# First mixer of a two-block kernel: the order of front, inverse, solve, chain and norm for head pairs 1 to 3

## The chip, the core and the metric

The kernel runs on one core of a Trainium2 chip. The metric is the device time of one execution in microseconds, as the median of several runs; lower is better.

## What is computed

The program runs two transformer blocks over 512 tokens of width 1024. The first block has a mixer (a bidirectional RWKV-7 recurrence over 8 heads of 64, plus a pooling branch) and an expert layer; the second has another mixer and two feed-forward layers. Only the recurrence of the first mixer is touched:

```python
def step(state, inp):
    r_t, w_t, k_t, v_t, kk_t, a_t = inp
    sa = jnp.einsum('bhvk,bhk->bhv', state, -kk_t)
    state = (state * w_t[:, :, None, :]
             + sa[..., :, None] * (kk_t * a_t)[..., None, :]
             + v_t[..., :, None] * k_t[..., None, :])
    out = jnp.einsum('bhvk,bhk->bhv', state, r_t)
    return state, out
```

It is run forward and backward in time (d = 0 and 1), the two outputs are added and normalised per head, a bonus term is added, the sum is gated, and w_out projects the result together with the pooling branch.

## The kernel before, in words

The recurrence is not stepped token by token. The 8 heads are four pairs (i = 0 to 3, two heads of 64 rows in 128 partitions), the 512 tokens are 8 chunks of 64, and each pair goes through five functions:

- `front(i)` (line 348) loads r, k, v of the pair (line 355) and a low-rank weight (line 358), normalises k (`head_scale`, lines 326 to 343: matmuls L330 and L343), makes the decay and the mixing gates (L371, L373), scans the decay within chunks (L385), and for each direction makes scaled copies on VectorE and GpSimd (L392 to L405) and the small products within each chunk on TensorE (L318, called through `mm2`), which VectorE masks into the tiles `gl`, `kc` and `x` (L415, L428). Its last matmul is the bonus term (L431). Its PSUM tiles come from the pool `ppf`, which has two.
- `invert(i)` (line 435) inverts a triangular 64x64 matrix for each chunk, head and direction: a transpose on VectorE (L448), 15 dependent steps of a multiply and an add on VectorE (L469, L470), two more transposes (`dt` L473, `dn` L475), then five groups of small matmuls (L488, L495, L503, L510, L517), each with a ScalarE or VectorE copy before the next can start; the last copy is L521. It starts from `gl`, so from the end of its front. Its tiles (`inv`) and its PSUM tile (`ppi`) exist once.
- `solve(i)` (line 523) turns v (L318 on `v` and `vf`, copied at L537), applies the inverse (`x<-th`, L545), and folds the result into `kc` and `rd` (L551, L557); last comes the part of each chunk that does not depend on the state (L562, L563). PSUM from `ppb`, two tiles.
- `chain(i)` (line 565) carries the state through the 8 chunks: per chunk one matmul group into `pzs`, one VectorE add (L585), one group into `po`. `po` is one of the two `ppb` tiles and is held to the end; `pzs` exists once.
- `back(i)` (line 589) copies `po` (L596), centres and normalises it (L598, `head_scale` again) and applies the gate.

The tiles that a pair carries from one function to the next (`gl`, `rd`, `x`, `kc`, `at`, `th`) live in one of three slots, pair i in slot i % 3. Slots 1 and 2 are opened at lines 624 and 625, after the 20 input projections (`w_in`, matmuls at L141), and closed after `back(2)`. The space they leave is used by the tile `xt` (loads at L643) and by the pool `wp3`: the pooling results `pd` (loads at L666, one buffer, four in turn, each split by ScalarE at L70 and GpSimd at L71), and the weights of the output projection. `project(4, 4)` (line 649) multiplies the four pooling tiles with w_out: 8 output blocks of 12 matmuls, 96 in all, at L141. `solve(3)`, `chain(3)` and `back(3)` are written between the pooling splits and this projection.

The program text is not the order on the engines. A planner lays out each engine's queue ahead of time: an instruction written earlier goes first when it is ready, and one written later fills in when nothing earlier is ready and its tiles are free. What it lays out is then fixed; each engine works through its queue in order. So moving a call in the text moves priorities, and the trace shows what filled in where.

Of the kernel before, what the change touches and what calls it, by code (L numbers as in the profile page):

```python
# [40 lines left out]
def flip(ap):  # L41
    dims = [list(q) for q in ap.ap]
    step, n = dims[-1]
    dims[-1] = [-step, n]
    return bass.AP(tensor=ap.tensor, offset=ap.offset + step * (n - 1), ap=dims)
# [3 lines left out]
def tile_two_blocks(ctx: ExitStack, tc: tile.TileContext, a: dict, out: bass.AP):  # L49
# [15 lines left out]
    def vv(name, j):  # L65
        o = VOFF[name] + j
        return vec[:, o:o + 1]
# [95 lines left out]
    with ExitStack() as c1:  # L163
# [9 lines left out]
        def psb(p=ppb):  # L173
            return p.tile([128, 512], F32, tag="ps", name="ps")
# [133 lines left out]
        def open_slots(n, side):  # L308
            c = c1.enter_context(ExitStack())
            slots[n] = (mk(c, f"slot{n}", 1, side=side), c)  # L310

        def c8(ap):
            return ap.rearrange("p (c t) -> p c t", t=64)

        def mm2(ps, w_, x_, start=True, stop=True):

            for j in (0, 64):
                PE.matmul(ps[j:j + 64], w_[j:j + 64], x_[j:j + 64], start=start, stop=stop, tile_position=(j, j))  # L318

        def c4(ps):  # L320
            return ps.rearrange("p (c t) -> p c t", t=128)
# [4 lines left out]
        def head_scale(pp, sq, eps):  # L326

            ps = psb(pp)
            for t in range(4):
                PE.matmul(ps[:, t * 2:t * 2 + 2], sq[:, t * 128:(t + 1) * 128], cst[:, C_IND:C_IND + 2],  # L330
                          start=True, stop=True)
            rs = tp.tile([128, 2, 8], F32, tag=f"rs{eps is None}", name="rs", bufs=2)
            if eps is None:
                S.activation(rs[:, 0], ps[:, :8], AF.Sqrt)
                V.tensor_scalar(rs[:, 0], rs[:, 0], 1e-12, None, op0=ALU.max)
            else:
                V.tensor_scalar(rs[:, 0], ps[:, :8], 1.0 / 64, eps, op0=ALU.mult, op1=ALU.add)
                S.activation(rs[:, 0], rs[:, 0], AF.Sqrt)
            V.reciprocal(rs[:, 1], rs[:, 0])
            pb = psb(pp)  # L340
            for t in range(4):
                for j in range(2):
                    PE.matmul(pb[j * 64:j * 64 + 64, t * 128:(t + 1) * 128],  # L343
                              rs[:, 1, t * 2 + j:t * 2 + j + 1].to_broadcast([128, 64]), ident,
                              start=True, stop=True)
            return pb
# [176 lines left out]
        def solve(i):  # L523


            qd = Q[i]
            th, gl = qd["th"], qd["gl"]

            vt = qd["vt"] = gl[:, :, :, 64:128]
            vT = rkv["v", i]  # L530
            vf = tp.tile([128, T], F32, tag="vf", name="vf")
            G.tensor_copy(vf, flip(vT))
            for d in range(2):
                p = c8(psb())
                for c in range(8):
                    mm2(p[:, c, :], c8(vf if d else vT)[:, c, :], ident2)
                S.activation(vt[:, d], p, AF.Copy)  # L537
            for d in range(2):
                u = qd[d]
                rd, x_, kc, at_ = u["rd"], u["x"], u["kc"], u["at"]  # L540
                for h in range(2):
                    p = c4(psb())
                    for c in range(4):
                        mm2(p[:, c, :], th[:, h * 4 + c, d, :], x_[:, h * 4 + c, :])
                    S.activation(x_[:, h * 4:h * 4 + 4], p, AF.Copy)  # L545
                for h in range(2):
                    cs_ = slice(h * 4, h * 4 + 4)
                    p = c4(psb())
                    for c in range(4):
                        mm2(p[:, c, :], gl[:, d, h * 4 + c, 0:64], x_[:, h * 4 + c, :])  # L550
                    V.tensor_add(kc[:, cs_], kc[:, cs_], p)  # L551
                    p = c4(psb())
                    c0 = 1 - h
                    cs_ = slice(h * 4 + c0, h * 4 + 4)
                    for c in range(c0, 4):
                        mm2(p[:, c, :], at_[:, h * 4 + c, :], x_[:, h * 4 + c, :])
                    V.tensor_add(rd[:, cs_], rd[:, cs_], p[:, c0:])  # L557

                p = c8(psb())
                for c in range(7):  # L560
                    mm2(p[:, c, :], kc[:, c, 64:128], vt[:, d, c, :])
                S.activation(th[:, 1, d, :], p[:, 0, :], AF.Copy)  # L562
                S.activation(gl[:, d, 1:7, 0:64], p[:, 1:7, :], AF.Copy)  # L563

        def chain(i):
            qd = Q[i]
            th = qd["th"]
            po = qd["po"] = psb()

            def out_(c, d, inter):  # L570
                n = 7 - c if d else c
                r_ = qd[d]["rd" if inter else "kc"][:, c, 0:64]
                mm2(po[:, n * 64:n * 64 + 64], th[:, c, d, :] if inter else qd["vt"][:, d, c, :],
                    flip(r_) if d else r_, start=not inter and c == 0 and d == 0, stop=inter and c == 7 and d == 1)

            for c in range(8):
                for d in range(2):
                    out_(c, d, False) if d == 0 else out_(7 - c, d, False)
            pzs = ppz.tile([128, 2, 2, 64], F32, tag="pz", name="pzs")
            for c in range(7):  # L580
                if c:
                    pz = pzs[:, c % 2]
                    for d in range(2):
                        mm2(pz[:, d], qd[d]["rd"][:, c, 64:128], th[:, c, d, :])
                    V.tensor_add(th[:, c + 1], pz, qd["gl"][:, :, c, 0:64])  # L585
                for d in range(2):
                    out_(c + 1, d, True)

        def back(i):
            qd = Q.pop(i)  # L590
            po = qd["po"]

            gt = tp.tile([128, T], F32, tag="gt", name="gt")
            nc.sync.dma_start(gt, gate_d[i])
            o = yt[i] = yb.tile([128, T], F32, tag="y", name="y") if i < 3 else tp.tile([128, T], F32, tag="nkk", name="y")
            S.activation(o, po, AF.Copy)  # L596
            pb = psb()
            PE.matmul(pb, cst[:, C_CEN:C_CEN + 128], o, start=True, stop=True)  # L598
            S.activation(o, pb, AF.Copy)
            sq = tp.tile([128, T], F32, tag="vf", name="sq")  # L600
            S.activation(sq, pb, AF.Square)
            pb = head_scale(ppb, sq, 64e-5)
            V.tensor_mul(o, o, pb)
            V.tensor_scalar(o, o, vv("ln_x_w", i), vv("ln_x_b", i), op0=ALU.mult, op1=ALU.add)
            V.tensor_add(o, o, qd["bon"])
            V.tensor_mul(o, o, gt)
# [16 lines left out]
        cw.close()  # L623
        open_slots(1, "right")
        open_slots(2, "right")
        front(1)
        invert(1)
        front(2)
        solve(1)
        chain(1)  # L630
        invert(2)
        back(1)
        front(3)
        solve(2)
        chain(2)
        invert(3)
        back(2)
        slots[2][1].close()
        slots[1][1].close()
        xp = mk(cx1, "xp3", 1, side="right")  # L640
# [832 lines left out]
```

## Time and profile before

| what | value |
|---|---|
| median of 3 runs | 3052.63 us (3047.12 to 3056.36) |
| profiled execution | 3042.29 us, span 3040.5 us |
| TensorE busy over the span | 2877.7 us (95%) |
| VectorE busy over the span | 1896.8 us (62%) |
| stretch of pairs 1 to 3, up to the end of `project(4, 4)` | about 223 to 443 us |
| TensorE busy in that stretch | 188.15 of 220 us |

All times in views are microseconds from the span's start. PE is TensorE, PEld its weight loads, DVE VectorE, ACT ScalarE, POOL GpSimd, SP the queue that issues most DMAs. A tile such as `ps<-x,th` reads: the matmul wrote ps from x and th. "[idle before <-X]" is how long the engine stood still before the row and what ended that. The granted clock (PEclk) is 1.00 at the full 2.4 GHz and 0.50 at 1.2 GHz; between them it is a mean over the stretch.

### The profile page before, as it was taken

How to read it: one execution, taken by the hardware profiler on the slowest of the kernel's cores; microseconds unless marked ns; L12 is line 12 of the kernel's file. 1: busy time of each engine (PE TensorE's matmuls, PEld its weight loads, DVE VectorE, ACT ScalarE, POOL GpSimd, SP SyncE). 2: the span in 40 equal slices, each digit the busy share in tenths (PEclk: the TensorE clock that was granted, in tenths of full speed). 3: DMA queues.
4: the chain of work that ended last, by engine and by line, in shares of the span. 5: the costliest groups of instructions: out<-in, count | busy, mean ns of one | idle time of the engine just before them, and what ended most of it. 6: DMA issues, size and time to landing. Idle time of an engine off the chain costs nothing.

```text
span 3040.5 us, 45240 instructions
## 1 busy us (share of the span) xinstructions
PE 2877.7 (95%) x17733; PEld 2402.8 (79%) x17733; DVE 1896.8 (62%) x3317; ACT 1198.8 (39%) x2073; POOL 924.9 (30%) x584
## 2 busy tenths in 40 slices
PE   8897898999989799999999999999999999999998
PEld 6676776799989677799999977888876666788886
DVE  7567638899987377777777786332258744643311
ACT  6344334237867233333333334332234343433322
POOL 1011135211321111133444324444431233244443
PEclk9899989999999899999999999999999999999999
DMA  3240123257876699999899962333321112323332
GB/s 115 63 129 27 41 77 122 70 164 257 315 271 241 239 303 318 311 327 306 307 315 332 313 218 63 97 97 95 99 93 49 56 56 66 101 91 97 97 96 78
DMA packets 201286, 494.92 MB, mean 163 GB/s; under 512 B 17328, under 2 KB 95152, under 8 KB 199152
## 3 DMA queue, kind: packets, MB, share of 16 engines
q1 hardware_dynamic: 164208, 357.78, 36.0%
q0 software_dynamic: 36864, 134.23, 12.7%
q8 instruction: 140, 2.29, 0.3%
q14 instruction: 74, 0.61, 0.1%
HBM read 446.60 MB, written 45.22 MB: 162 GB/s over the span
## 4 chain that ended last, share of the span: by engine, by line
PE 59%; DVE 21%; issue 7%; ACT 4%; DMA 4%; POOL 2%; SPq 0%; ACTq 0%; DVEq 0%; POOLq 0%
PE ps L141 33%; PE pss L731 8%; PE pv L1043 8%; DVE vl L978 2%; DVE row L756 2%; ACT vh L972 2%; DVE o L913 2%; PE ps L318 2%; DVE ul L71 2%; DMA gate<-gates_d 2%; DMA uraw<-peer_ut 1%; PE po L1287 1%; DVE st L983 1%; PE pg L920 1%; PE ps L1263 1%
## 5 line engine op out<-in xcount | busy, mean ns | idle before, releaser
L71 POOL TENSOR_TENSOR wlo<-wraw,whi 128x1024 fp32r<-128x1024 f32 (+4 forms) x232 | 503.6, 2174 | 775.9 <-ACT whi L70 773.7
L70 ACT ACTIVATE whi<-wraw 128x1024 fp32r<-128x1024 f32 (+4 forms) x320 | 261.7, 823 | 692.2 <-PE ps L141 428.6
L750 POOL DMA_INDIRECT row<-peer_u,idx x128 | 158.1, 1235 | 618.2 <-DVE row L756 427.6
L141 PE MATMUL ps<-lo,whi 128*128 128x512 f32 x1112 | 303.4, 402 | 2.3 <-DVE pad L218 1.4
L141 PE MATMUL ps<-hi,whi 128*128 128x512 f32 x1112 | 295.1, 395 | 0.0
L141 PE MATMUL ps<-hi,wlo 128*128 128x512 f32 x1112 | 293.9, 395 | 1.1 <-POOL wlo L71 0.7
L141 PEld LDWEIGHTS ps<-lo,whi 128*128 128x128 f32 x1112 | 208.1, 190 | 55.6 <-issue 11.0
L1043 PE MATMUL pv<-vl,gh 128*128 128x512 f32 x768 | 243.1, 398 | 6.8 <-DVE vl L978 4.3
L141 PEld LDWEIGHTS ps<-hi,wlo 128*128 128x128 f32 x1112 | 208.0, 189 | 51.5 <-issue 6.3
L750 POOL DMA_INDIRECT row<-peer_v,idx x128 | 168.6, 1317 | 256.7 <-DVE acc L761 219.3
L141 PEld LDWEIGHTS ps<-hi,whi 128*128 128x128 f32 x1112 | 207.6, 188 | 47.1 <-issue 5.2
L1043 PE MATMUL pv<-vh,gl 128*128 128x512 f32 x768 | 239.0, 392 | 1.9 <-ACT vh L972 1.9
L1043 PE MATMUL pv<-vh,gh 128*128 128x512 f32 x768 | 239.6, 393 | 0.0
L70 ACT ACTIVATE gh<-st 128x384 fp32r<-128x384 f32 x128 | 67.2, 525 | 414.2 <-DVE st L983 224.2
L731 PE MATMUL pss<-lo,uh 128*128 128x384 f32 x1024 | 210.5, 347 | 17.6 <-ACT st L735 17.4
L731 PE MATMUL pss<-hi,ul 128*128 128x384 f32 x1024 | 203.4, 339 | 4.0 <-DVE ul L71 4.0
L731 PEld LDWEIGHTS pss<-lo,uh 128*128 128x128 f32 x1024 | 183.2, 192 | 23.6 <-ACT st L735 19.2
L731 PE MATMUL pss<-hi,uh 128*128 128x384 f32 x1024 | 199.5, 336 | 0.0
L978 DVE TENSOR_TENSOR vl<-vraw,vh 128x1024 fp32r<-128x1024 f32 x128 | 161.4, 1261 | 50.1 <-ACT vh L972 49.7
L71 DVE TENSOR_TENSOR ul<-uraw,uh 128x1024 fp32r<-128x1024 f32 x128 | 156.2, 1220 | 53.3 <-ACT uh L70 53.3
L731 PEld LDWEIGHTS pss<-hi,ul 128*128 128x128 f32 x1024 | 182.6, 191 | 4.7 <-DVE ul L71 4.7
L1043 PEld LDWEIGHTS pv<-vl,gh 128*128 128x128 f32 x768 | 141.4, 189 | 52.0 <-DVE vl L978 23.6
(445 smaller groups left out, 5236.6 us busy)
## 6 DMA issues: line engine op xcount, KB each, us to landing
uraw<-peer_ut SPq DMA_DIRECT2D x128, 512.0 KB, 6.2
vraw<-peer_v SPq DMA_DIRECT2D x128, 512.0 KB, 5.5
wraw<-ffn_w_in SPq DMA_DIRECT2D x88, 512.0 KB, 3.5
gates_d<-stg SPq DMA_DIRECT2D x12, 2048.0 KB, 9.2
gate<-gates_d SPq DMA_DIRECT2D x32, 768.0 KB, 8.1
wraw<-w_in SPq DMA_DIRECT2D x40, 512.0 KB, 3.5
wraw<-ffn_w_out SPq DMA_DIRECT2D x32, 512.0 KB, 3.5
st_d<-st SPq DMA_DIRECT2D x58, 192.0 KB, 4.2
```

Source lines behind the costliest of these rows:

```text
L70: S.activation(hi, src, AF.Copy)
L71: eng.tensor_sub(lo, src, hi)
L141: PE.matmul(ps, w_[:, k, :m], x_[:, k0 + k, :], start=n == 0, stop=n == last)
L318: PE.matmul(ps[j:j + 64], w_[j:j + 64], x_[j:j + 64], start=start, stop=stop, tile_position=(j, j))
L731: PE.matmul(ps, w_[:, k, :], x_[:, k, :ND], start=n == 0, stop=n == 23)
L750: G.indirect_dma_start(out=r, out_offset=None, in_=tab, in_offset=bass.IndirectOffsetOnAxis(ap=idx[:, i:i + 1], axis=0))
L756: V.scalar_tensor_tensor(r, r, 1.0, htok, op0=ALU.mult, op1=ALU.mult, accum_out=act[:, s:s + 1])
L913: V.tensor_tensor(oo[n], io[:, None, :].to_broadcast([128, 8, 128]), tr[:, n, t0:t0 + 8, None].to_broadcast([128, 8, 128]), op=ALU.is_equal)
L920: PE.matmul(pg[:, i, :], oo[1][:, e + i, :], oo[0][:, e + i, :], start=True, stop=True)
L972: S.activation(vh, vld[b], AF.Copy)
L978: V.tensor_sub(vl, raw, vh)
L1043: PE.matmul(pv[t * 2 + e], l_[:, ts_], r_[:, e * 512:(e + 1) * 512], start=b == 0 and q == 0, stop=b == 127 and q == 2)
```

## The change

```diff
         open_slots(2, "right")
-        front(1)
-        invert(1)
-        front(2)
-        solve(1)
-        chain(1)
-        invert(2)
-        back(1)
-        front(3)
-        solve(2)
-        chain(2)
-        invert(3)
-        back(2)
+        for i in range(1, 4):
+            front(i)
+            invert(i)
+        for i in range(1, 3):
+            solve(i)
+            chain(i)
+            back(i)
         slots[2][1].close()
```

The same calls are made, each once. `front(1)`, `invert(1)` and `front(2)` stay the first three. Behind them `invert(2)`, `front(3)` and `invert(3)` now come ahead of `solve(1)`, `chain(1)`, `back(1)`, `solve(2)`, `chain(2)` and `back(2)`. Nothing inside a function changes, and `solve(3)`, `chain(3)`, `back(3)` stay where they were.

## Rows read from the trace of the kernel before

**Rows 1.** Page, part 1: busy us, share of the span, instructions of each engine

```profile
PE 2877.7 (95%) x17733; PEld 2402.8 (79%) x17733; DVE 1896.8 (62%) x3317; ACT 1198.8 (39%) x2073; POOL 924.9 (30%) x584
```

**Rows 2.** Busy time by stretch: length, PE, PEld, DVE, ACT, POOL, PEclk, DMA

```profile
246.00:279.50 33.50, 22.10 (x607) 16.98 (x607) 26.28 (x54) 18.26 (x27) 8.82 (x9) 0.85 0.11 27
...
279.50:380.00 100.50, 88.05 (x1958) 74.30 (x1954) 69.85 (x145) 34.44 (x58) 11.63 (x11) 0.93 0.11 36
...
292.00:358.50 66.50, 58.72 (x1266) 48.57 (x1264) 44.36 (x89) 26.17 (x43) 10.19 (x10) 0.92 0.14 46
...
380.00:413.00 33.00, 29.55 (x689) 26.58 (x683) 9.40 (x14) 17.47 (x32) 9.62 (x8) 0.84 0.30 90
```

**Rows 3.** What TensorE waited for, 223 to 279 us: total, times, longest

```profile
PE ps L488 <- DVE dt L473: 7.1, 1, 7.1
```

**Rows 4.** Timeline of TensorE: heads and ends of fronts 2 and 3

```profile
245.84 0.95 PE L330 MATMUL ps<-cst,sq 128*128 128x2 f32 x8
...
279.63 2.28 PE L318 MATMUL ps<-x,th 64*64 64x128 f32 x31
...
290.63 1.10 PE L431 MATMUL ps<-r__2899,rbo 128*128 128x512 f32 x2 [1.16 <-DVE kc L428]
...
292.67 1.05 PE L330 MATMUL ps<-cst,sq 128*128 128x2 f32 x8
...
319.69 0.44 PE L343 MATMUL ps<-ident,rs 128*64 128x128 f32 x4
...
357.03 1.10 PE L431 MATMUL ps<-r__3773,rbo 128*128 128x512 f32 x2 [1.05 <-DVE kc L428]
```

**Rows 5.** Timeline of ScalarE: the last copy of inverses 1, 2 and 3

```profile
278.70 1.20 ACT L521 ACTIVATE th<-ps 32x512 f32<-32x512 f32 x2 [0.69 <-PE ps L517]
...
331.66 1.19 ACT L521 ACTIVATE th<-ps 32x512 f32<-32x512 f32 x2 [0.35 <-PE ps L517]
...
392.69 1.19 ACT L521 ACTIVATE th<-ps 32x512 f32<-32x512 f32 x2 [2.22 <-PE ps L517]
```

**Rows 6.** Timeline of TensorE: inverse groups, chain 2, solve 3, first projections

```profile
274.95 1.20 PE L510 MATMUL ps<-tn,gl 32*32 32x32 f32 x64
...
367.76 2.08 PE L318 MATMUL ps<-kc,gl 64*64 64x64 f32 x64
...
379.74 0.45 PE L318 MATMUL ps<-rd,th 64*64 64x64 f32 x8
...
386.14 1.92 PE L510 MATMUL ps<-tn,gl 32*32 32x32 f32 x64
...
389.89 0.90 PE L318 MATMUL ps<-cst,v 64*64 64x64 f32 x10
...
413.13 0.96 PE L141 MATMUL ps<-pl,whi 128*128 128x512 f32 x3
```

**Rows 7.** Timelines of SP's queue and GpSimd: loads into freed slots, last pooling split

```profile
318.01 1.93 SPq L643 DMA_DIRECT2D xt<-xT  x4
...
380.16 0.33 SPq L666 DMA_DIRECT2D pd<-pooled_d  x1
...
405.68 1.27 POOL L71 TENSOR_TENSOR pl<-pd,ph 128x512 fp32r<-128x512 f32 x1 [3.40 <-ACT ph L70]
```

**Rows 8.** Chain of waits, 412 to 448 us: the rest of project(4, 4)

```profile
428.28 14.54 PE ps L141 x63
```

**Rows 9.** Timelines of VectorE and GpSimd inside inverse 1, and GpSimd after it

```profile
246.65 0.21 DVE L470 TENSOR_TENSOR tr<-tr,tm 128x56 f32<-128x56 f32 x1
...
258.14 1.16 DVE L470 TENSOR_TENSOR tr<-tr,tm 128x56 f32<-128x56 f32 x1
...
261.63 1.98 DVE L475 STREAM_TRANSPOSE dn<-tr 128x1024 f32<-128x1024 f32 x1
...
256.62 2.61 POOL L405 TENSOR_TENSOR r__2899<-at,r 128x512 f32<-128x512 f32 x1 [9.90 <-issue]
...
271.25 1.26 POOL L405 TENSOR_TENSOR r__3001<-at,r 128x512 f32<-128x512 f32 x1 [0.76 <-DVE at L402]
```

## The prediction

> **What bounds the kernel now.** I read the busy times of the page first: TensorE is busy for 95% of the span [rows 1], so what a stretch can give is the time in which TensorE stands still or runs at half clock there. All the change moves lies between 246 and 443 us. The table by stretch [rows 2] shows that this is TensorE's weakest part: 22.10 of 33.50 us busy in 246 to 279.5, 88.05 of 100.50 in 279.5 to 380, 29.55 of 33.00 in 380 to 413, at mean clocks of 0.85, 0.93 and 0.84. The hole of the first stretch is inverse 1, whose VectorE steps leave TensorE 7.1 us without work [rows 3]. The next view is the timeline, for where each pair's steps begin and end. Front 2 goes from its head at 245.84 to its last matmul at 291.73, 45.9 us, with inverse 1 beside it. Front 3 begins its head at 292.67, has it done only at 320.1, because solve 1, chain 1 and inverse 2 are written ahead of it, and ends at 358.13: 65.5 us [rows 4]. Inverse i ends with a ScalarE copy at 279.90, 332.85 and 393.88 [rows 5]. Solve 3 has to wait for the last of these and starts at 389.89 [rows 6].
>
> One more wait sets the end. The first pooling load goes out at 380.16 [rows 7], the moment chain 2 gives its last matmul group back (379.74 + 0.45 [rows 6]): its space is that of slot 2. From there to the end of the fourth pooling split, at 406.95, are 26.8 us [rows 7], and the projection's matmuls run from 413.13 [rows 6] to 442.82 [rows 8]. So three things order the end: when inverse 3 is done, when chain 2 is done, and how much TensorE has to do in between.
>
> **The change, part by part.** No instruction is added or removed. What moves is priority.
>
> 1. *Up to 279.5 us: nothing.* The first three calls are the same, and solve 1's matmuls already run as filler between those of front 2 (279.63 [rows 4]), so what is behind them was not keeping them busy. Inverse 1's 7.1 us hole stays.
>
> 2. *Front 3.* It starts where it did, since its head uses the two PSUM tiles that front 2 gives back at 291.7. With only inverse 2 ahead of it, it stands as front 2 did beside inverse 1, so I take that one's 45.9 us: end at 338.6 in place of 358.1, 19.5 us earlier. From below it can't take more than its old 65.5 us.
>
> 3. *Inverse 3.* From the end of its front to its last copy an inverse took 34.1 us (pair 1, from 245.84 on, where front 2's head followed front 1's last matmul), 41.1 (pair 2, behind solve 1 and chain 1) and 35.8 (pair 3) [rows 4, 5]. It now has no solve ahead of it; with 35 it ends at 373.5, 20 us earlier than 393.9.
>
> 4. *Chain 2.* Here the change pays back. Up to chain 2's end at 380.2 TensorE did 88.05 us of work since 279.5 and stood still for 12.45 [rows 2]. All of it must still be done, and inverse 3's last three groups, which used to come behind, now come first: 3 x 1.20 = 3.6 us at full clock [rows 6]. Without any idle time chain 2 would end at 279.5 + 91.7 = 371.2, with the old idle time at 383.6. Fronts and inverses feed TensorE in bursts and the solves of pairs 1 and 2 are there to fill, so I take half, 6.8 us: 378.
>
> 5. *The pooling splits*, 26.8 us behind chain 2 [rows 7]: 404.8. Solve 3 starts at 373.5, takes its old 23.2 us up to the first projection (389.89 to 413.13 [rows 6], half-clock groups in it) and shares TensorE with chain 2 and back 2 for about 4 us; chain 3's steps are the 12.4 us of chain 2 (367.76 to 380.19) less its opening of 2.1 [rows 6]. So chain 3 ends near 411, with the projection already filling between its steps. Nothing waits for it longer than that.
>
> 6. *The projection.* 63 of its matmuls took 14.54 us [rows 8], 0.231 each; the 95 from 413.13 on need 21.9 us, and the 29.7 us they took had 7.8 us of chain 3 and back 3 between them. Part of that is done before 404.8 now. Bounds 21.9 and 29.7, middle 26: end at 430.8.
>
> 7. *GpSimd beside the inverse.* In inverse 1 one add of a step took 1.16 us at 258.14 where the same size took 0.21 at 246.65, while GpSimd's multiply of front 2 took 2.61 in place of 1.26 [rows 9]. Front 3's GpSimd work now falls into inverse 2's steps. I charge one such hit, 1.0 us: 431.8. The Trainium skill, SBUF - State Buffer, section Who interferes with whom, says that a VectorE instruction with two SBUF inputs contends with a GpSimd instruction that reads SBUF, the loser standing still for the whole instruction. The trace agrees, with 1.16 against 0.21 us; by the rule each of front 3's five larger GpSimd operations could hit like this one, some 5 us in place of 1 (an estimate).
>
> 8. *DMAs.* The loads of front 3 stay where they are, ahead of everything. `xt`, which waits for chain 1 (318.01 [rows 7]), comes later and is needed only at the first projection. It shares SP's queue with the identity that inverse 3 starts from; if they are queued the wrong way round, inverse 3 starts as much later as chain 1 ends after inverse 2, a few us. I take nothing, as chain 1's rest is short by then; the upper bound of step 6 has room for it.
>
> Sum: the projection ends at 431.8 instead of 442.8, 11.0 us earlier. Behind it the order is the old one and TensorE-bound, so the gain reaches the end. Against the profiled execution that is 3042.3 - 11.0 = 3031.3. That execution lies 10.3 us below the median of the three runs, so on the median it is 3052.6 - 11.0 = **3041.6 us**. With the bounds of 4 and 6 the case's own gain goes from 2 us (383.6 + 26.8 + 29.7 = 440.1, +1) to 20 (371.2 + 26.8 + 24 = 422), so 3032.6 to 3050.6.
>
> **The rivals.**
>
> *It was full already: no change.* Chain 2's end moves back by what is put ahead of it, and the idle time stays. Then chain 2 ends at 383.6 or a little later and the pooling splits, which gate the projection, start later than before. For it: 88% of 279.5 to 380 was busy, and the planner already filled by readiness, so the text may not have held anything up. Against it: front 3's head, ready at 293, was finished at 320. A gain of -2 to 2 us: 3050 to 3055.
>
> *VectorE becomes the bound: slower.* Place: 292 to 357 us. VectorE was busy 44.36 us from 292 to 358.5 [rows 2]. Inverse 3's steps and transposes move into the same stretch; inverse 1's lasted 17.8 us (245.84 to 263.61 [rows 4, 9]) with instructions of front 2 among them, so I add some 12 us: 56 of 65 us. Solve 1's, chain 1's and solve 2's adds now stand behind all of these. If chain 1 is not done before inverse 3's transposes end, at about 357 (in inverse 1 that was 16.3 us before its last copy, 263.6 [rows 9] to 279.9), solve 2 finds only one of the two PSUM tiles (chain 1 holds the other), comes behind it, and solve 2 (23 us as solve 3's row) with chain 2 (12.4) and inverse 3's five groups (some 7) follow one another: 357 + 42 = 399; pooling and projection put the end at 399 + 26.8 + 27 = 452.8, 10 us slower: 3063. It decides from chain 2's end at 390 on (442.8 - 26 - 26.8). Against it: chain 1 has from about 310 on, and its adds are small. The Trainium skill, Perfetto Trace Analysis, section Optimization Strategy, advises interleaving regimes in which different engines are the most contended, and this change groups them instead; by that advice the old order was the better one, and the time would go this way.
>
> *More than the idle time: the clock.* The mean clock of 0.84 in 380 to 413 [rows 2] goes with groups of 1.92 us at 386.14 against 1.20 at 274.95 [rows 6]. If the stretch is filled so well that it stays at full clock, the groups of that stretch give back some 9 us more: gain 20 to 24, about 3030.
>
> **How the numbers follow.** About 0.3%, 9.2 us, is what a measurement of this kernel can tell from no change. The forecast gets 0.60, no change 0.18, the slower case 0.13, the clock 0.09. Of the forecast's gains of 2 to 20 us somewhat over three fifths lie above 9.2 us, so faster is 0.37 + 0.09 = 0.46. The rest of it, the second case and 0.02 of the slower one give 0.43 within the bound; slower keeps 0.11. The range holds the forecast's own range and the no-change case, and leaves out the clock case and most of the slower one: 3032 to 3056, 0.80.
>
> **What would show it.** Right: front 3's bonus matmul at 336 to 342, inverse 3's last copy before 378, the first pooling load at 374 to 382, the last projection matmul of this group at 428 to 436. Step 2 is wrong if front 3's head is again stretched over more than 10 us; step 4 if the first pooling load comes after 384; step 5 if TensorE waits after chain 3 with the pooling splits still to come. The prediction is wrong as a whole if that load comes after 390, or if the stretch ends earlier and the total does not follow.

## The result and the profile after

The changed kernel took 3065.4 us (median of 7 runs, 3061.6 to 3073.7), the kernel before 3049.3 us beside it (7 runs, 3044.0 to 3056.4). The ratio is 1.0052 [1.0039, 1.0066]: **slower by 0.52%, about 16 us**, where 11 us faster was forecast.

The profiled execution took 3073.7 us, 8 above its median, and that of before [rows 1] lies 7 below the 7-run median. The two profiles thus show more of a difference than the medians do. The page of the changed kernel, part 1:

```profile
PE 2900.7 (94%) x17733; PEld 2419.4 (79%) x17733; DVE 1897.0 (62%) x3317; ACT 1198.6 (39%) x2073; POOL 924.3 (30%) x584
```

The instructions are the same in number, as forecast, and TensorE is busy 23 us longer with them. The table by stretch, columns as in [rows 2], answers to the four rows there:

```profile
246.00:279.50 33.50, 22.40 (x510) 16.92 (x512) 26.05 (x55) 15.83 (x23) 8.82 (x9) 0.76 0.08 26
...
279.50:380.00 100.50, 85.61 (x1900) 72.07 (x1902) 64.11 (x132) 39.98 (x64) 10.31 (x11) 0.79 0.10 34
...
292.00:358.50 66.50, 53.47 (x1159) 43.75 (x1154) 52.94 (x116) 25.31 (x40) 9.70 (x10) 0.90 0.04 10
...
380.00:413.00 33.00, 27.80 (x502) 24.69 (x500) 9.79 (x20) 8.62 (x19) 4.95 (x5) 0.86 0.18 54
```

From 292 to 358.5 VectorE went from 44.36 us to 52.94, and TensorE fell from 58.72 to 53.47. That is the work the change brought together: steps of inverses on VectorE, while TensorE has less to do. The clock is lower as well, 0.79 against 0.93 over 279.5 to 380.

Where does the stage end? A fixed mark is the first matmul behind it, at L154 (`ps<-lu,whi`, the next layer's weight `wq`): 471.46 before, 492.89 after. From 279.5 to that mark the table by stretch of the kernel before says

```profile
279.50:471.46 191.96, 171.44 (x2932) 140.30 (x2929) 99.01 (x192) 68.74 (x121) 49.74 (x43) 0.92 0.21 64
```

and that of the changed kernel

```profile
279.50:492.89 213.39, 184.61 (x3029) 152.73 (x3029) 101.84 (x193) 71.11 (x125) 48.70 (x43) 0.85 0.19 58
```

The stretch is 21.4 us longer: 13.2 us more TensorE busy and 8.2 us more idle (28.78 less 20.52). The 97 further matmuls had run ahead of 279.5 before; counted from 223 on, where the two are 1 us apart, 3863 matmuls after stand against 3858 before, and take 225.67 us against 212.19. So the 13 us more are the same matmuls at a lower clock, 0.85 against 0.92 in these rows.

Part of this lies ahead of anything that the change moves: front 2 already ends 6.3 us later (298.06 against 291.73). From front 2's end to the mark every one of these kernels runs the same 2750 matmuls or so. The table by stretch for the kernel before, the changed kernel, and two that are explained below, the changed kernel with own tiles and with slots swapped:

```profile
291.73:471.46 179.73, 160.43 (x2750) 131.09 (x2751) 90.30 (x178) 62.87 (x112) 48.47 (x42) 0.91 0.22 66
...
298.06:492.89 194.83, 167.19 (x2751) 136.98 (x2750) 92.03 (x178) 62.72 (x112) 47.41 (x42) 0.86 0.20 60
...
289.93:477.36 187.43, 159.82 (x2752) 130.06 (x2750) 91.23 (x178) 63.32 (x112) 46.95 (x41) 0.92 0.20 63
...
291.46:475.80 184.34, 162.44 (x2751) 131.27 (x2750) 90.15 (x178) 62.95 (x112) 47.19 (x42) 0.89 0.21 64
```

Here the change costs 15.1 us, close to the 16 of the medians: 6.8 us are the same matmuls at a lower clock (0.86 against 0.91), and 8.3 us are idle time (27.64 against 19.30).

The timeline of TensorE shows the order of events, bonus matmuls (L431, end of fronts 2 and 3) and opening groups of solves and chains, in the changed kernel:

```profile
296.96 1.10 PE L431 MATMUL ps<-r__2899,rbo 128*128 128x512 f32 x2 [1.14 <-DVE kc L428]
...
345.83 1.13 PE L431 MATMUL ps<-r__3462,rbo 128*128 128x512 f32 x2 [1.03 <-DVE kc L428]
...
349.33 2.03 PE L318 MATMUL ps<-kc,gl 64*64 64x64 f32 x64
...
364.66 2.08 PE L598 MATMUL ps<-y,cst 128*128 128x512 f32 x2
...
377.44 1.97 PE L318 MATMUL ps<-cst,v 64*64 64x64 f32 x32
...
394.54 2.08 PE L318 MATMUL ps<-kc,gl 64*64 64x64 f32 x64
...
402.81 0.45 PE L318 MATMUL ps<-rd,th 64*64 64x64 f32 x8 [0.39 <-DVE th L585]
...
410.57 1.97 PE L318 MATMUL ps<-cst,v 64*64 64x64 f32 x32
```

Read `ps<-kc,gl` as the opening of a chain and `ps<-cst,v` as the start of a solve. Two rows of the same view before:

```profile
303.84 2.08 PE L318 MATMUL ps<-kc,gl 64*64 64x64 f32 x64
...
328.25 0.91 PE L318 MATMUL ps<-cst,v 64*64 64x64 f32 x22
```

Front 3 ends 11.2 us sooner (345.83 against 357.03 [rows 4]), so the change does what it says. But chain 1 opens 45 us later (349.33 against 303.84), solve 2 starts 49 us later (377.44), chain 2 opens 27 us later (394.54 against 367.76 [rows 6]) and ends at 403.3 in place of 380.2. The pooling load goes out with that end; SP's queue after:

```profile
403.22 0.34 SPq L661 DMA_DIRECT2D pd<-pooled_d  x1
```

Inverse 3 was done well before, as ScalarE's timeline after shows, next to the end of inverse 2 (compare [rows 5]):

```profile
334.55 1.19 ACT L521 ACTIVATE th<-ps 32x512 f32<-32x512 f32 x2 [1.30 <-PE ps L517]
...
376.94 1.19 ACT L521 ACTIVATE th<-ps 32x512 f32<-32x512 f32 x2 [2.56 <-PE ps L517]
```

It ends at 378.1, 16 us sooner than before, and solve 3, for which this was to be done, starts at 410.57: 21 us **later** than before (389.89 [rows 6]). What lies between is seen in the chain of waits of the changed kernel, from 345 to 412 us (start, length, what):

```profile
375.04 1.85 PE ps L517 x64
...
377.51 7.08 PE ps L318 x112
384.61 0.70 DVE kc L551
385.36 6.29 PE ps L318 x120
391.78 5.07 PE ps L318 x132
397.08 0.30 DVE th L585
397.43 0.45 PE ps L318 x8
398.16 0.30 DVE th L585
```

As soon as inverse 3's last group is out, solve 2 runs alone from 377.5 to 394.5, then chain 2 alternates with VectorE's adds. Both were to fill the gaps of front 3 and inverse 3 and fill nothing. One of the tiles that solve 2 needs is `vf`; the row in GpSimd's timeline after shows what that waited for:

```profile
371.43 0.61 POOL L532 COPY vf<-v 128x512 f32<-128x512 f32 x1 [27.01 <-PE ps L330]
```

`vf` is a tile that exists once and that `back(1)` uses too, for the squares that its sum at L330 reads. Solve 2 can copy into it only when that sum is done, and `back(1)` waits for chain 1. Only the second of solve 2's two opening groups reads `vf`; the first reads `v` and needs a `ppb` tile, and chain 1 and `back(1)` come ahead of it for those in the order of the text. Which of the two tiles came last is not shown; both wait for `back(1)`. The table by stretch in steps of 20 us shows the price on either side:

```profile
300.00:320.00 20.00, 13.01 (x128) 8.54 (x128) 19.07 (x45) 11.16 (x15) 3.67 (x4) 0.86 0.00 1
...
340.00:360.00 20.00, 15.36 (x320) 12.78 (x319) 16.91 (x45) 3.59 (x7) 1.29 (x1) 0.88 0.01 2
360.00:380.00 20.00, 19.14 (x522) 16.09 (x513) 5.01 (x9) 9.59 (x16) 0.61 (x1) 0.50 0.29 108
```

In 300 to 320 VectorE is full (19.07 of 20) and TensorE has 7 us without work; in 340 to 360 it is 4.6 us. Then, from 360 to 380, TensorE is busy 19.14 us at a granted clock of 0.50.

### The profile page after: what moved, and what is told of

Same layout as the page of the kernel before. It is cut to its first block, busy times and chain, and to the rows that moved or that the text cites. A ratio compares the mean times of both kernels' runs of the same rounds, so it can differ in the third digit from the quotient of the medians.

```text
span 3071.9 us, 45241 instructions
## 1 busy us (share of the span) xinstructions
PE 2900.7 (94%) x17733; PEld 2419.4 (79%) x17733; DVE 1897.0 (62%) x3317; ACT 1198.6 (39%) x2073; POOL 924.3 (30%) x584
## 4 chain that ended last, share of the span: by engine, by line
PE 57%; DVE 21%; issue 7%; ACT 5%; DMA 4%; POOL 2%; SPq 0%; ACTq 0%; DVEq 0%; POOLq 0%
PE ps L141 32%; PE pv L1038 8%; PE pss L726 7%; PE ps L318 3%; DVE vl L973 2%; DVE row L751 2%; ACT vh L967 2%; DVE o L908 2%; DMA uraw<-peer_ut 2%; DMA gate<-gates_d 2%; DVE ul L71 1%; POOL wlo L71 1%; PE po L1282 1%; DVE st L978 1%; PE ps L1258 1%
## 5 line engine op out<-in xcount | busy, mean ns | idle before, releaser
L726 PE MATMUL pss<-lo,uh 128*128 128x384 f32 x1024 | 209.9, 346 | 17.5 <-ACT st L730 16.5
```

What stands on the lines that cost most here:

```text
L726: PE.matmul(ps, w_[:, k, :], x_[:, k, :ND], start=n == 0, stop=n == 23)
```

## The experiments

**The theory.** Solve, chain and back of a pair form a train: they hand two tiles on to each other in the order of the text, one of the two `ppb` PSUM tiles (held by a chain to its end) and `vf`. So solve 2 cannot overtake chain 1 and back 1, whatever is ready. The change puts three bursts ahead of the first train, the trains leave late and one behind the other, and the pooling loads (and so the projection) leave with the second. **Rivals:** VectorE's load from 292 to 358 us is the bound by itself; the priority costs by itself, without the tiles; or work put ahead breaks up the interleaving and costs half-clock time, as the first expectations have it.

The first two medians are of 7 executions each; every other one is of 11 or 12, beside 35 of the kernel before on the same chip (3047.8 to 3048.4 us). The ratios are the better comparison, as the kernels did not all run on the same chip. "Stage end" is the mark from above in the one profiled execution of the kernel, which lies up to 8.3 us from the kernel's median.

| kernel | chain 2 ends | stage end | median us | ratio |
|---|---|---|---|---|
| before | 380.2 | 471.5 | 3049.3 | 1 |
| changed | 403.3 | 492.9 | 3065.4 | 1.0052 [1.0039, 1.0066] |
| inverse 2 ahead alone | 379.5 | 470.8 | 3047.4 | 1.0000 [0.9985, 1.0015] |
| inverse 3 ahead alone | 387.9 | 479.7 | 3057.4 | 1.0025 [1.0009, 1.0041] |
| inverse 2 and front 3 ahead | 390.3 | 479.6 | 3057.9 | 1.0032 [1.0018, 1.0046] |
| changed, own tiles | 389.2 | 477.4 | 3056.4 | 1.0029 [1.0016, 1.0043] |
| before, own tiles | 383.7 | 475.9 | 3051.1 | 1.0006 [0.9990, 1.0021] |
| changed, slots swapped | 398.7 | 475.8 | 3054.2 | 1.0027 [1.0012, 1.0041] |
| before, slots swapped | 383.3 | 465.3 | 3045.9 | 0.9991 [0.9974, 1.0008] |
| changed, both | 390.1 | 473.6 | 3053.0 | 1.0016 [1.0003, 1.0029] |
| before, both | 392.2 | 481.7 | 3057.5 | 1.0037 [1.0023, 1.0051] |
| chain 2 ahead of front 3 | 355.9 | 463.8 | 3044.0 | 0.9987 [0.9973, 1.0000] |
| the same, own tiles | 359.3 | 466.3 | 3041.7 | 0.9988 [0.9974, 1.0001] |
| front 3 between solve 2 and chain 2 | 375.0 | 473.7 | 3046.9 | 0.9999 [0.9985, 1.0013] |

The profiled execution's own time less its stage end lies between 2570.8 and 2581.4 us in all fourteen rows, while the stage ends spread over 29 us. Differences of more than 10 us are thus settled before that mark; smaller ones can't be placed in this way.

### Which of the moved calls costs

Only `invert(2)` ahead of the first train:

```diff
         front(2)
+        invert(2)
         solve(1)
         chain(1)
-        invert(2)
```

> Order: front 1, inverse 1, front 2, inverse 2, solve 1, chain 1, back 1, front 3, solve 2, chain 2, inverse 3, back 2. Only inverse 2 is put ahead of solve 1, chain 1 and back 1; the rest is as before. Theory (a train): solve, chain and back of pairs 1, 2 and 3 follow one another through the same few tiles (two PSUM tiles of ppb, one of which is held by the chain; vf), so the end moves with the departure of this train, the end of solve 1 (its opening of chain 1 at 303.8 us before, at 349.3 after). Inverse 2 alone delays it by a few us: 3048 to 3055. Rival 1 (TensorE is simply full, so what is put ahead costs its own matmul time): inverse 2 is 7 of the 37 us put ahead, so a fifth of the loss, 3 us: 3052. Rival 2 (any group put ahead breaks the interleaving and costs half-clock time): 3057 to 3063.

1.0000: this part is free (the theory had a few us for it). Solve 2 starts later (340.0 against 328.2 in its trace), but chain 2 ends where it did.

Only `invert(3)` ahead of the second train:

```diff
         front(3)
+        invert(3)
         solve(2)
         chain(2)
-        invert(3)
```

> Order: front 1, inverse 1, front 2, solve 1, chain 1, inverse 2, back 1, front 3, inverse 3, solve 2, chain 2, back 2. Only inverse 3 is put ahead of solve 2 and chain 2. Theory (train): solve 1 and chain 1 leave as before (chain 1 opens at 304 us), solve 2 begins where it did since it needs back 1's tiles; inverse 3 ahead of solve 2 costs 0 to 5 us: 3047 to 3055. Then the loss lies in front 3 ahead of solve 1. Rival 1 (full TensorE): a fifth, 3 us: 3052. Rival 2 (breaking up the interleaving with inverse 3 is what costs): 3057 to 3065.

It costs about 8 us by itself, where the theory had 0 to 5; the median lies in the range of the rival of broken interleaving. TensorE's timeline of this kernel in chain 2:

```profile
366.05 2.08 PE L318 MATMUL ps<-kc,gl 64*64 64x64 f32 x64
...
380.43 1.92 PE L503 MATMUL ps<-p,dn 32*32 32x32 f32 x64
...
384.39 1.92 PE L510 MATMUL ps<-tn,gl 32*32 32x32 f32 x64
...
387.32 0.69 PE L318 MATMUL ps<-rd,th 64*64 64x64 f32 x8 [0.39 <-DVE th L585]
387.94 1.92 PE L517 MATMUL ps<-th,tn 32*32 32x32 f32 x64
```

Chain 2 opens as before (366.05 against 367.76) and then takes 21.9 us instead of 12.4, since inverse 3's groups are laid between its steps, at 1.92 us each where 1.20 is the full-clock time [rows 6]. So here half-clock time is a part of the price, as that rival has it; the two parts are not separated. Inverse 3 itself is done only 3 us sooner (389.9 against 392.7 for its last matmuls).

`invert(2)` and `front(3)` ahead of the first train, `invert(3)` where it was:

```diff
         front(2)
+        invert(2)
+        front(3)
         solve(1)
         chain(1)
-        invert(2)
         back(1)
-        front(3)
```

> Order: front 1, inverse 1, front 2, inverse 2, front 3, solve 1, chain 1, back 1, solve 2, chain 2, inverse 3, back 2. Front 3 and inverse 2 are ahead of solve 1 and chain 1, inverse 3 is behind chain 2 as before. Theory (train): the delay of solve 1 behind front 3 is most of the loss; chain 1 opens at 330 us or later, chain 2 ends at 390 to 403, and the rest of the stage follows some 90 us behind that, as in all five profiles so far: 3055 to 3065. Rival: the loss is inverse 3 in front of solve 2 and chain 2 (3057 when only that was put ahead), and front 3 costs nothing: 3046 to 3051.

About 10 us. In its trace chain 1 opens at 345.4 instead of 303.8, right behind front 3's end, and chain 2 at 380.8. So `front(3)` ahead of the first train costs about as much as `invert(3)` ahead of the second, and both together, the change, 16.

### The tiles that couple the trains

In the changed kernel, `po` and the PSUM tiles of `back` for pairs 1 and 2 come from `ppw`, the input projections' pool, which is idle here; the squares of `back(1)` go into the dead tile `at`, so `vf` is free for solve 2:

```diff
+        def pq(i):
+            return ppw if i in (1, 2) else ppb
...
-            po = qd["po"] = psb()
+            po = qd["po"] = psb(pq(i))
...
-            pb = psb()
+            pb = psb(pq(i))
...
-            sq = tp.tile([128, T], F32, tag="vf", name="sq")
+            sq = tp.tile([128, T], F32, tag="vf", name="sq") if i != 1 else qd[0]["at"].rearrange("p c t -> p (c t)")
...
-            pb = head_scale(ppb, sq, 64e-5)
+            pb = head_scale(pq(i), sq, 64e-5)
```

> The changed kernel, with the train's couplings loosened: chain 1 and 2 hold a PSUM tile of the idle pool ppw in place of one of ppb, back 1 and 2 take their PSUM tiles there too, and back 1's squares go into a dead tile of its own pair in place of vf. Nothing else moves. Theory (train): solve 2 no longer waits for back 1 (it began at 377 us after the change), but can begin when inverse 2 is done, at about 336, as filler of front 3, inverse 3 and chain 1; chain 2 ends 15 to 25 us sooner than its 403, and the time comes back to that of the kernel before or below: 3040 to 3052. Rival 1 (full TensorE: the order of priorities alone sets the time) and rival 2 (grouping lowers the clock): the same as the changed kernel within 4 us, 3061 to 3070.

The same edit in the kernel before:

> The kernel before with the same three tiles loosened and its own order. Theory (train): its solve 2 began at 328 us right behind back 1, and inverse 2 was done at 333, so little is held up there; solve 3 began at 389.9 and inverse 3 was done at 393.9, again little: 0 to 6 us faster, 3043 to 3050. Rivals: no change, 3047 to 3052.

With its own tiles the changed kernel gains 7 us by the ratios (1.0029 against 1.0052) and 9 by the medians, less than the theory had, and ends between its range and the rivals'; the kernel before gains nothing (1.0006). The edit loosens `vf` and the PSUM tiles at once, so their shares are not separated. TensorE's timeline of the changed kernel with own tiles:

```profile
341.17 1.92 PE L318 MATMUL ps<-kc,gl 64*64 64x64 f32 x60
...
343.26 0.63 PE L318 MATMUL ps<-cst,v 64*64 64x64 f32 x16
...
380.65 1.92 PE L318 MATMUL ps<-kc,gl 64*64 64x64 f32 x60
```

Solve 2 now runs between the steps of chain 1 (343.26, not 377.44), and chain 2 opens at 380.65, 14 us sooner. For solve 2's start this tells the theory from the VectorE rival: VectorE still has 49.8 us of work from 292 to 358.5. Yet chain 1 is as late as front 3 makes it (341.17), and the kernel stays slower than before by 0.29%. How much of chain 1's delay is VectorE's load is not tested.

The gain is also not the one that the theory describes. In the four rows from front 2's end on, the changed kernel stands idle for 27.64 us and the one with own tiles for 27.61; the 7.4 us between them are matmuls at a clock of 0.92 in place of 0.86. Solve 2 thus ran earlier without filling idle time, and the time came back through the clock. With one profiled execution of each, whether the tiles bring this clock every time stays open.

### The pooling loads

Slots 1 and 2 trade places, opened and closed in the other order, so that the pooling loads wait for chain 1 and `xt` for chain 2; first in the kernel before, then in the changed one:

```diff
-        open_slots(1, "right")
         open_slots(2, "right")
+        open_slots(1, "right")
...
-        slots[2][1].close()
         slots[1][1].close()
+        slots[2][1].close()
```

> The kernel before with slots 1 and 2 opened and closed in the other order, so that the space under the pooling loads is slot 1's, free when chain 1 is done, and the space under xt is slot 2's. Theory (the end waits for chain 2 because the pooling loads do): the loads go out at about 318 us in place of 380, the pooling splits are done long before chain 2, and the projection's matmuls start as soon as xt has landed, about 390, or fill before; the stage ends 8 to 20 us sooner: 3029 to 3041. Rival (the projection waits for solve 3, chain 3 and a full TensorE anyway): 3044 to 3051.

> The changed kernel with slots 1 and 2 opened and closed in the other order. Theory: the pooling loads go out when chain 1 is done, at about 362 us in place of 403; the projection has its operands when solve 3 and chain 3 run and is done some 10 to 20 us sooner: 3045 to 3055. Rival: chain 2's end holds the projection in another way (xt, which now waits for it), and the train as a whole is late: 3060 to 3068.

In the kernel before the first load goes out at 313.1 instead of 380.2, and the time doesn't move (0.9991), where the theory had 8 to 20 us. So it was not the loads alone that held the end there. In the changed kernel (first load 355.6) the same edit gives back 8 us by the ratios, 11 by the medians, within the theory's range: there the late loads did cost. Its row from front 2's end on has 5.7 us less idle time than the changed kernel's (21.90 against 27.64) and 4.8 us less busy time.

Both edits together, in the changed kernel and in the kernel before:

> The changed kernel with both couplings loosened: the train's own tiles (which took 9 of its 16 us) and the swapped slots (which took 11 of them). Theory: the change costs its 16 us by two couplings and nothing else, that solve 2 waits for back 1 and that the pooling loads wait for chain 2; without both it is no slower than the kernel before, 3038 to 3050. Rival 1 (both undo the same loss, as the first makes chain 2 earlier and the second makes it matter less): 3052 to 3058, as each alone. Rival 2 (priorities on a full TensorE cost something by themselves): 3050 to 3056.

> The kernel before with both couplings loosened (alone: 3051 and 3046 against 3048). Theory: neither bound it, since its train left in time, so nothing comes of both: 3043 to 3052. Rival (one hid the other): 3034 to 3042.

In the changed kernel 11 to 12 of the 16 us come back, less than the two gains together: in part the couplings cover the same delay from two ends. The theory had all of it (3038 to 3050); 3053.0 lies in the ranges of both rivals. A rest of 0.16% [0.03%, 0.29%] stays, which the order may cost without any tile. I don't claim that, since the kernel before with both edits became slower by 0.37%, which neither theory expected. In its trace chain 2 opens at 377.6, ten us late, and inverse 3 ends at 406. Why the plan came out so is open; edits to tiles that ought to be neutral can thus move this stage by 10 us, which limits how far the rest, and single steps of this size, can be read.

The runs also let the two orders be compared with the same edit in both, as the difference of two ratios. The changed order costs 0.52% with the tiles as they were, 0.23% with own tiles, 0.36% with slots swapped, and with both edits it is 0.21% faster (1.0016 against 1.0037). So the cost is not one that the order has whatever the tiles are; how much of the last figure is the slow plan of the kernel before with both edits is open.

### The other way round

If the train sets the end, it should go first: `front(3)` and `invert(3)` behind chain 2.

```diff
         back(1)
-        front(3)
         solve(2)
         chain(2)
+        front(3)
         invert(3)
```

> Order: front 1, inverse 1, front 2, solve 1, chain 1, inverse 2, back 1, solve 2, chain 2, front 3, inverse 3, back 2: the opposite of the change, the train of pairs 1 and 2 ahead of front 3. Theory (the end follows chain 2's end by some 90 us): chain 2 ends at 350 to 368, the pooling loads go out then, and the stage ends 5 to 15 us sooner: 3034 to 3044. Rival (then pair 3 becomes the late one: front 3, inverse 3, solve 3, chain 3 and back 3 follow one another behind, and only the projection fills them): 3046 to 3062.

3044.0 us, 0.9987 [0.9973, 1.0000]: about 4 us faster than before, at the edge of what can be told and of the theory's range, and some 20 us faster than the changed kernel. Its table by stretch, for the stretch that VectorE crowded:

```profile
292.00:358.50 66.50, 59.89 (x1454) 50.14 (x1453) 41.07 (x86) 25.75 (x45) 9.44 (x8) 1.00 0.17 54
```

TensorE is busy 59.89 us at a clock of 1.00, against 53.47 at 0.90 in the changed kernel. SP's queue:

```profile
355.92 0.33 SPq L666 DMA_DIRECT2D pd<-pooled_d  x1
```

The pooling loads go out 24 us sooner than before, but little of this is left at the stage's end (463.8 against 471.5): front 3's bonus matmul now ends at 374.7 and inverse 3's last at 406.0, so that the end waits for pair 3 instead.

With its own tiles as well, and with `front(3)` between `solve(2)` and `chain(2)`:

> The order with solve 2 and chain 2 ahead of front 3 (3044 against 3048), with the train's tiles loosened too. Theory: with the train in front nothing of it waits for a tile any more (solve 2 began 9 us after back 1's first matmul, and inverse 2 was done at 329), so it gains nothing: 3040 to 3047. Rival (solve 3 waits for back 2's tiles, as back 2 is the last of the text): 3034 to 3040.

> Front 3 between solve 2 and chain 2: order front 1, inverse 1, front 2, solve 1, chain 1, inverse 2, back 1, solve 2, front 3, chain 2, inverse 3, back 2. Theory (two late ends to balance: chain 2 for the pooling loads, inverse 3 for solve 3): chain 2 ends near 365 in place of 356, inverse 3 near 398 in place of 407; the stage ends 0 to 5 us sooner than with front 3 behind chain 2: 3038 to 3045. Rival (chain 2's small steps are the filler that front 3 needs, and putting front 3 ahead of them costs as it did for chain 1): 3046 to 3052.

The first is no different from the order alone (0.9988 against 0.9987), as expected. The second is no different from before (0.9999), where the theory had 3038 to 3045: this points to chain 2 itself as what has to be ahead of front 3, but its interval [0.9985, 1.0013] overlaps that of the order alone, so it is not shown.

## Why the prediction was wrong

- **Step 1** held for the order, but not for the profiled time: front 2's bonus matmul came at 296.96, 6.3 us later than in [rows 4], though TensorE's groups were in the same order up to there.
- **Steps 2 and 3** were right in size. Front 3's bonus matmul ended at 347.0 instead of 338.6, 6 us of which are the late start; with own tiles it ended at 338.8, with slots swapped at 340.9. Inverse 3's last copy ended at 378.1 instead of 373.5. From its front's end inverse 3 took 31.2 us, less than the 35 of the sum. But solve 3 could not use it.
- **Step 4 failed.** It took TensorE's work and idle time as one sum that any ready matmul may fill, and put chain 2's end at 378 with bounds of 371.2 and 383.6; it came at 403.3. "The solves of pairs 1 and 2 are there to fill" is the sentence that was wrong. Solve 1's end stood behind front 3, and solve 2 had neither `vf` nor a second PSUM tile until `back(1)` was through. So solve 2 and chain 2 ran behind the bursts, alone, from 377.5 on. The own tiles give back 7 to 9 us; `front(3)` ahead alone costs 10, with an overlap. The step also priced TensorE's work at the old clock: the 91.7 us of work and 6.8 of idle time in its sum became 106.27 us and 17.5 from 279.5 to 403.3, at a clock of 0.82 in place of 0.93 (97 of these matmuls had run before 279.5 in [rows 2]). Why the clock fell is open.
- **Step 5** was right in its rule: the first load went out at 403.22, as chain 2 ended. From there to the stage end are 89.7 us, before 91.3. Hence what was lost at chain 2 was lost at the end.
- **Step 6** had no chance to show, as chain 3 came behind the loads: solve 3 started 7 us after the first. Its range was not summed as written either: the gain of 20 us takes 24 for the projection where the step's bound is 21.9, which would have made it 22.
- **Step 7** was too small. Two adds of inverse 2 were hit, in VectorE's timeline:

```profile
302.32 0.27 DVE L470 TENSOR_TENSOR tr<-tr,tm 128x110 f32<-128x110 f32 x1
...
310.09 1.31 DVE L470 TENSOR_TENSOR tr<-tr,tm 128x110 f32<-128x110 f32 x1
...
313.73 1.10 DVE L470 TENSOR_TENSOR tr<-tr,tm 128x78 f32<-128x78 f32 x1
```

and each beside an instruction of front 3 in GpSimd's timeline:

```profile
310.01 1.26 POOL L405 TENSOR_TENSOR r__3462<-at,r 128x512 f32<-128x512 f32 x1 [11.24 <-ACT en L387]
313.67 1.06 POOL L395 TENSOR_TENSOR rd<-cst,e 128x512 f32<-128x512 f32 x1 [2.40 <-ACT e L390]
```

Each add ends within 0.2 us of the GpSimd instruction beside it. This agrees with the Trainium skill, SBUF - State Buffer, section Who interferes with whom, by which such an add contends with a GpSimd instruction that reads SBUF. The free add of the first size took 0.27 us, at 302.32, so the two hits cost about 1.9 us instead of 1.0. The five hits that the prediction worked out from the Trainium skill's rule, some 5 us, did not come.
- **Step 8** held: `xt` went out at 362.4 and nothing waited for it.

**The rivals.** The slower one, with a chance of 0.13, came nearest. Its event came as written: chain 1's last group ran at 361.66, when inverse 3's transposes had just ended (in the chain of waits the second starts at 359.59 and takes 1.88), and solve 2 fell behind inverse 3. It put chain 2's end at 399 and the time at 3063; they were 403 and 3065. VectorE had 52.94 us in 66.5, where 56 in 65 was forecast. What it had wrong is its name, as far as solve 2 goes: with VectorE nearly as full, own tiles let solve 2 start 34 us earlier, so the tile decides there, not the engine. For chain 1, 45 us late and still as late with own tiles, VectorE's load is not ruled out: VectorE was busy 19.07 us of the 20 from 300 to 320. The Trainium skill's advice to interleave regimes (Perfetto Trace Analysis, section Optimization Strategy), quoted there against this change, has the direction that was measured: the change cost 0.52%. No run shows that grouping is the reason: inverse 2 ahead was free, and own tiles gave time back with the grouping as it was. "Full already" fell with the 8 us of new idle time, and the clock rival went the other way: 0.85 from 279.5 to the stage end, against 0.92. The clock was in the forecast at no price, and from front 2's end on it took 6.8 of the 15.1 us.

The chances were wrong in one respect that the profile of before could have shown. Which tiles a waiting function needs, and who holds them in the text's order, was asked for solve 2 in the slower rival alone, and priced there as a matter of VectorE; it belonged in step 4.

## What to carry to other kernels

Before a piece of work is counted as filler, list the buffers it needs and who holds them in the order of the text: work that shares a single tile with its predecessor cannot fill, however ready its data is. In a stage that ends with a serial train, ask when the last train leaves and what leaves with it; an earlier start of what comes behind it (here inverse 3, 16 us sooner) was worth nothing. Here the serial part first, with the bursts around it, gave the lowest medians (3044.0 and 3041.7), at the edge of what can be told from before.

## What was not expected of the hardware

The granted clock differs between executions of kernels whose groups are still in the same order. From 273 to 288 it was 0.54 after and 1.00 before, with TensorE busy nearly all the time in both (15.00 and 14.85 of 15 us); front 2 ended 6 us apart. The table by stretch after, then before:

```profile
273.00:288.00 15.00, 15.00 (x288) 13.97 (x284) 3.96 (x6) 6.01 (x10) 1.65 (x2) 0.54 0.24 72
...
273.00:288.00 15.00, 14.85 (x381) 13.42 (x376) 6.92 (x11) 9.81 (x17) 1.07 (x2) 1.00 0.22 66
```

The mean from 246 to 279.5 (0.76 and 0.85) doesn't tell this: with inverse 3 ahead alone it was 0.75, and front 2 ended at 291.5. In the timeline after, front 2's groups and inverse 1's run at half clock:

```profile
275.18 2.40 PE L318 MATMUL ps<-rd,kb 64*64 64x128 f32 x20
277.51 1.92 PE L510 MATMUL ps<-tn,gl 32*32 32x32 f32 x64
```

The second is the group that took 1.20 us at 274.95 before [rows 6]; the first took 1.31 there, at 273.60. This is a part of the profiles' 21 us that the order need not answer for. The clock fell later as well: busy 19.14 of 20 us with small groups of norms and inverse 3, TensorE still ran from 360 to 380 at 0.50, after 20 us in which it was busy for 15.36. A busy TensorE is thus no sign of full clock in such stretches.

An in-order queue also charged a wait that no step had listed. The waits of TensorE after, from 279 to 464 us (total, times, longest), have

```profile
PE pzs L318 <- ACT th L562: 4.4, 1, 4.4
```

The copy at L562 that this waits for stood in ScalarE's queue behind table loads of front 3's functions:

```profile
307.73 1.28 ACT L387 ACT_TABLE_LOAD   x1
...
309.67 1.28 ACT L373 ACT_TABLE_LOAD   x1
...
311.67 1.28 ACT L390 ACT_TABLE_LOAD   x1
```

So solve 1, laid in as filler, held up TensorE's queue for 4.4 us, because its small copy came behind three loads of 1.28 us and the activations that they served. The kernel with `front(3)` ahead alone has the same wait, also 4.4 us.
